# SwiGLU's upward products by seven half-depth products for two weight blocks and two token halves

## The chip, the cores and the metric

The kernel runs on one core of one Trainium2 chip. The metric is device time in microseconds (us) of one execution. Weights are read from device memory in every execution.

## The reference, cut to what matters

The program is one inference step of a two-layer decoder trunk, all in float32. There are 576 tokens: 512 of a prompt and 8 sequences of 8. Each layer has a SwiGLU block (FFN), a mixer and a second FFN; the model width is 1024 and the inner width of an FFN 2816.

```python
def swiglu(h, w1, w3, w2):
    return (jax.nn.silu(h @ w1) * (h @ w3)) @ w2

for l in range(DEPTH):                      # 2 layers
    ada = silu(c) @ w_ada + b_ada           # shift, scale, gate x 3
    h = modulate(rms_norm(x, g_ffn1), sh1, sc1)
    x = x + 0.5 * gt1 * swiglu(h, w1_a, w3_a, w2_a)
    h = modulate(rms_norm(x, g_mix), sh2, sc2)
    x = x + gt2 * mixer(h)                  # retention, two convolutions, gates
    h = modulate(rms_norm(x, g_ffn2), sh3, sc3)
    x = x + 0.5 * gt3 * swiglu(h, w1_b, w3_b, w2_b)
```

The change touches `h @ w1` and `h @ w3` of the four FFNs.

## The kernel before

Activations lie transposed: a tile has 128 features by 576 tokens, and the width of 1024 is eight such tiles, `self.h`. Tokens are worked in two halves of `HB` = 288 columns. Every float32 operand is held as a pair `hi`, `lo` of the type fp32r: `hi` is a rounded copy, made on ScalarE (ACT), and `lo` the rest, a subtraction on VectorE (DVE). A product is then three matmuls, `hi`·`hi`, `hi`·`lo` and `lo`·`hi`, into one PSUM bank (`three`, L210 to L212; the activations' `lo` comes second).

A weight block is 128 x 1024: 128 output features, all eight depth tiles beside each other. It has 48 matmuls: 8 depth tiles x 2 token halves x 3. An FFN has `FT` = 22 pairs of blocks upward, one of `w1` and one of `w3`; `post` forms silu of the first times the second, and splits the result into `ghi`, `glo`. After each of three `GROUPS` of pairs (6, 8 and 8), eight blocks of `w2` carry the group's part downward and add it to `x` (`residual`). The first pairs of an FFN are worked in `begin` (or `begin_first`), woven into the end of the normalisation before.

The order of work is written out by hand: `self.steps` is a list of steps with the weight blocks that each uses, and each engine carries out its instructions in the order in which the steps issue them. `pump` looks ahead in the list of weights: it issues the load of a raw block (on SP's queue) while fewer than `RAW` raw buffers are held, and splits the next raw block, ACT's copy (L161) and DVE's subtraction (`rest`, L121), while fewer than `WB` = 5 pairs of buffers are live and the block is at most `AHEAD` = 4 weight blocks away. It is called from `use`, and from `tick` between products. `spare` blocks are split into general slots instead. In the first and the second FFN, units of the matrix `w_ada` (two loads and eight matmul records a unit) are put between the steps (`add_fill`), with up to `ADA` = 12 of their loads ahead. GpSimd (POOL) adds the residual of the 64 sample tokens (L590) and takes small parts of the normalisation and the mixer.

## Time and profile before

| | |
|---|---|
| median of 3 runs | 3166.7 us (3166.56 to 3167.11) |
| the profiled execution's own time | 3166.99 us |
| its span, first to last instruction | 3165.2 us |
| TensorE matmul (PE) busy | 3104.3 us, 98% of the span |
| VectorE (DVE) busy | 1537.2 us, 49% |
| ScalarE (ACT) busy | 873.5 us, 28% |
| GpSimd (POOL) busy | 394.4 us, 12% |
| mean granted TensorE clock | 0.992 |

The profiled execution is one of the program on the chip. Busy time is the union of an engine's instructions. A matmul's record is longer than the distance to the next matmul, since they overlap; the number of matmuls in a stretch gives their distance. "PEld" is the load of a matmul's stationary operand.

### The profile page before, as it was taken

What the parts mean: (1) busy time and instruction counts of PE and PEld (TensorE: products, weight loads), DVE (VectorE), ACT (ScalarE), POOL (GpSimd) and SP (SyncE); (2) the same over time, 40 slices, a digit from 0 to 9 for tenths busy, and PEclk for the clock granted to TensorE, in tenths of its full rate; (3) what the DMA queues carried; (4) which work ended last, traced back from release to release, by engine and by line L of the source; (5) the groups of instructions that cost most, each with busy time, mean ns of one, the idle gap of its engine ahead of it and who ended that gap; (6) DMA issues with size and microseconds to landing.
All of it is one profiled execution on the core that took longest, in us unless ns stands there. A gap on an engine that the chain in (4) does not pass through costs nothing.

```text
span 3165.2 us, 55293 instructions
## 1 busy us (share of the span) xinstructions
PE 3104.3 (98%) x23412; PEld 2979.4 (94%) x23412; DVE 1537.2 (49%) x2840; ACT 873.5 (28%) x1468; POOL 394.4 (12%) x526
## 2 busy tenths in 40 slices
PE   7999999999999999999999999999998999999998
PEld 5999999899999999999999999988998999999998
DVE  5333336356985463323363333454579654533334
ACT  4222223222233342222232222332222333422221
POOL 1000004223112020000020000042221210200000
PEclk9999999999999999999999999999999999999999
DMA  7544423324222334636322222233342232222221
GB/s 274 166 154 150 150 94 123 110 75 117 72 84 84 107 121 136 208 133 212 112 80 78 86 86 86 85 118 113 89 112 64 83 101 89 77 85 85 81 81 57
DMA packets 142680, 349.67 MB, mean 110 GB/s; under 512 B 32400, under 2 KB 36752, under 8 KB 142432
## 3 DMA queue, kind: packets, MB, share of 16 engines
q1 hardware_dynamic: 135776, 329.35, 33.0%
q0 software_dynamic: 5504, 15.61, 1.8%
q8 instruction: 183, 3.00, 0.4%
q10 hardware_dynamic: 1152, 1.18, 0.1%
q14 instruction: 65, 0.53, 0.1%
HBM read 328.90 MB, written 12.45 MB: 108 GB/s over the span
## 4 chain that ended last, share of the span: by engine, by line
PE 87%; DVE 8%; POOL 2%; issue 1%; DMA 1%; ACT 1%; ACTq 0%; SPq 0%; DVEq 0%; POOLq 0%
PE pl L210 26%; PE pl L211 26%; PE pl L212 26%; DVE cv L957 4%; PE pm L277 2%; DVE lo L121 1%; PE pl L765 1%; PE pl L767 1%; PE pl L766 1%; PE pm L1164 1%; PE pm L1166 1%; DMA ada<-in_ada 1%; DVE cv L955 1%; DVE hl L383 0%; DVE t L393 0%
## 5 line engine op out<-in xcount | busy, mean ns | idle before, releaser
L210 PE MATMUL pl<-hh,hi 128*128 128x288 f32 x4576 | 1364.4, 298 | 9.3 <-DVE m L870 9.0
L211 PE MATMUL pl<-hl,hi 128*128 128x288 f32 x4576 | 1353.9, 296 | 10.1 <-POOL hl L421 9.6
L212 PE MATMUL pl<-hh,lo 128*128 128x288 f32 x4576 | 1353.1, 296 | 0.0
L210 PEld LDWEIGHTS pl<-hh,hi 128*128 128x128 f32 x4576 | 863.7, 189 | 32.3 <-DVE m L870 10.7
L211 PEld LDWEIGHTS pl<-hl,hi 128*128 128x128 f32 x4576 | 863.6, 189 | 12.7 <-POOL hl L421 10.9
L212 PEld LDWEIGHTS pl<-hh,lo 128*128 128x128 f32 x4576 | 863.4, 189 | 0.0
L121 DVE TENSOR_TENSOR lo<-raw,hi 128x1024 fp32r<-128x1024 f32 (+1 forms) x446 | 550.5, 1236 | 527.9 <-ACT hi L161 527.9
L161 ACT CAST hi<-raw 128x1024 fp32r<-128x1024 f32 (+1 forms) x446 | 459.0, 1032 | 845.5 <-PE pl L211 659.8
L210 PE MATMUL pl<-ghi,hi 128*128 128x288 f32 x1408 | 419.9, 298 | 0.0
L212 PE MATMUL pl<-ghi,lo 128*128 128x288 f32 x1408 | 415.2, 295 | 0.0
L211 PE MATMUL pl<-glo,hi 128*128 128x288 f32 x1408 | 415.1, 295 | 0.0
L210 PEld LDWEIGHTS pl<-ghi,hi 128*128 128x128 f32 x1408 | 264.4, 188 | 13.6 <-issue 11.5
L612 DVE TENSOR_TENSOR t<-t,pl 128x288 f32<-128x288 f32 x176 | 79.9, 454 | 404.7 <-PE pl L212 390.1
L590 POOL TENSOR_TENSOR xs<-xs,t 128x64 f32<-128x64 f32 x112 | 41.2, 368 | 1836.3 <-DVE t L587 1836.2
L211 PEld LDWEIGHTS pl<-glo,hi 128*128 128x128 f32 x1408 | 264.5, 188 | 0.0
L212 PEld LDWEIGHTS pl<-ghi,lo 128*128 128x128 f32 x1408 | 264.4, 188 | 0.0
L210 PE MATMUL pl<-s,hi 128*128 128x288 f32 x768 | 228.0, 297 | 1.9 <-DVE m L870 1.9
L211 PE MATMUL pl<-s,hi 128*128 128x288 f32 x768 | 226.6, 295 | 1.1 <-DVE s L226 1.1
L212 PE MATMUL pl<-s,lo 128*128 128x288 f32 x768 | 226.6, 295 | 0.0
L225 ACT CAST ghi<-t 128x288 fp32r<-128x288 f32 x176 | 76.1, 432 | 481.5 <-DVE t L612 481.5
L957 DVE SCALAR_TENSOR_TENSOR cv<-up,vec,cv 128x512 f32<-128x512 f32 x240 | 192.9, 804 | 5.4
L210 PEld LDWEIGHTS pl<-s,hi 128*128 128x128 f32 x768 | 144.4, 188 | 5.5 <-DVE m L870 2.4
(197 smaller groups left out, 2699.8 us busy)
## 6 DMA issues: line engine op xcount, KB each, us to landing
ada<-in_ada SPq DMA_DIRECT2D x288, 256.0 KB, 4.5
raw<-in_win SPq DMA_DIRECT2D x120, 512.0 KB, 3.6
raw<-in_w1a SPq DMA_DIRECT2D x44, 512.0 KB, 3.6
raw<-in_w3a SPq DMA_DIRECT2D x44, 512.0 KB, 3.6
raw<-in_w1b SPq DMA_DIRECT2D x44, 512.0 KB, 3.6
raw<-in_w3b SPq DMA_DIRECT2D x44, 512.0 KB, 3.6
raw<-in_w2a SPq DMA_DIRECT2D x32, 512.0 KB, 3.5
raw<-in_w2b SPq DMA_DIRECT2D x32, 512.0 KB, 3.5
```

Source lines behind the costliest of these rows:

```text
L121: self.nc.vector.tensor_sub(lo, t, hi.bitcast(F32))
L161: nc.scalar.copy(hi[:, :m], t[:, c])
L210: mm(ps[:, :HB], hi[:, c], x[0][:, t], start=first, stop=False)
L211: mm(ps[:, :HB], hi[:, c], x[1][:, t], start=False, stop=False)
L212: mm(ps[:, :HB], lo[:, c], x[0][:, t], start=False, stop=last)
L225: nc.scalar.copy(hi, src)
L277: nc.tensor.matmul(self.ps_ada[32 * j:32 * j + 32, :], self.cs[:, k], w, start=(k == 0), stop=(k == 7))
L590: nc.gpsimd.tensor_add(xs, xs, t[:].rearrange("p b t -> p (b t)"))
L612: nc.vector.tensor_mul(s, s, ps[1][:, :HB])
L765: mm(ps, xh, wh, start=(k == 0), stop=False)
L766: mm(ps, xh, wl, start=False, stop=False)
L957: nc.vector.scalar_tensor_tensor(cv[:, :S], up[:, k:k + S], w[:, k:k + 1], cv[:, :S], ALU.mult, ALU.add)
```

## The change

Two neighbouring weight blocks of the same kind and the two token halves are taken as a 2 x 2 by 2 x 2 product of blocks: weights by output block and by half of the depth, activations by half of the depth and by token half. Seven products of half depth (12 matmuls each) and sums before and behind them give what eight products of half depth (96 matmuls) gave.

- Pairs 0 and 1 stay as they were. Pairs 2 to 21 go two at a time through `duo_step`: `seven` for the two `w1` blocks, then `seven` for the two `w3` blocks. `GROUPS` are now 4, 6, 6 and 6 pairs.
- Weights: `sums` forms three sums from the raw blocks `a` and `b` on POOL (four adds of 128 x 512, and one of the four in a buffer `s1` of which there is one), and `halves` splits what came of them: X, Z and Y of 128 x 1024 and S of 128 x 512, each into one of the `WB` = 5 pairs of buffers. They are `jobs`, issued one at a time by `pump` when a pair of buffers is free.
- Activations: `forms` makes sums of the activations once for each FFN (POOL, DVE and ACT), `last_forms` overwrites a quarter of `hh`, `hl` with the last of them.
- Behind the products: `post` is called for each of the four results with one or two operands; sums on DVE, the three later products of the gate on POOL.
- Buffers: `RAW` 3 to 4, slots 38 to 37, temporary tiles 12 to 10; loads of `w_ada` ahead 12 to 4 after the start (`ADA_LATER`). `TAPS` in the mixer's convolution goes from 3, 1, 4 to 2, 2, 4; the mean in its norm uses another constant.

```diff
-GROUPS = ((0, 6), (6, 8), (14, 8))
+GROUPS = ((0, 4), (4, 6), (10, 6), (16, 6))
-RAW, WB, AHEAD, ADA = 3, 5, 4, 12
+RAW, WB, AHEAD, ADA, ADA_LATER = 4, 5, 4, 12, 4
-TAPS = 3, 1, 4
-SLOTS, TEMPS = 38, 12
+TAPS = 2, 2, 4
+SLOTS, TEMPS = 37, 10
...
-                if self.whole < ADA and self.n_dma <= self.cur + 2 * ADA:
+                if self.whole < (ADA if self.quota < 9 else ADA_LATER) and self.n_dma <= self.cur + 2 * ADA:
...
-            if self.raw and self.quota and self.order[self.raw[0][0]] <= self.order[self.cur] + AHEAD:
+            if self.jobs:
+                if self.live < WB:
+                    self.jobs.popleft()()
+                    if not later:
+                        self.rest()
+                    went = True
+            elif self.raw and self.quota and self.order[self.raw[0][0]] <= self.order[self.cur] + AHEAD:
                 key = self.keys[self.raw[0][0]]
                 spare = key in self.spare
-                if spare or self.live < WB:
+                if key in self.duo:
+                    if len(self.raw) > 1:
+                        self.sums(key, self.raw.popleft()[1], self.raw.popleft()[1])
+                        went = True
+                elif spare or self.live < WB:
...
+    def halves(self, key, t, n=1024):
+        w = [self.wp.tile([128, 1024], F32R, tag=x, bufs=WB, name=self.name(x)) for x in ("hi", "lo")]
+        self.live += 1
+        self.nc.scalar.copy(w[0][:, :n], t[:, :n])
+        self.late.append((w[1][:, :n], t[:, :n], w[0][:, :n]))
+        self.split[key] = w
+
+    def sums(self, key, a, b):
+        add = self.nc.gpsimd.tensor_add
+        s = self.wp.tile([128, 512], F32, tag="s1", bufs=1, name=self.name("s1"))
+        add(s, b[:, :512], b[:, 512:])
+        add(b[:, :512], b[:, :512], a[:, :512])
+        def z():
+            self.rest()
+            add(a[:, :512], a[:, :512], s)
+            add(a[:, 512:], a[:, 512:], a[:, :512])
+            self.halves((*key, "Z"), a)
+            self.held -= 1
+        def y():
+            self.halves((*key, "Y"), b)
+            self.held -= 1
+        self.jobs.extend((lambda: self.halves((*key, "X"), a), z, y, lambda: self.halves((*key, "S"), s, 512)))
+
+    def part(self, key, which):
+        self.cur = max(self.cur, self.at[key])
+        self.pump()
+        return self.split[(*key, which)]
...
+    def forms(self):
+        ...
+        for i in range(4):
+            za, zb = self.slot([128, NT], what="za"), self.slot([128, NT], what="zb")
+            nc.gpsimd.tensor_add(za, self.hh[:, i, :NT].bitcast(F32), self.hl[:, i].bitcast(F32))
+            nc.gpsimd.tensor_add(zb, self.hh[:, i + 4, :NT].bitcast(F32), self.hl[:, i + 4].bitcast(F32))
+            yield
+            a, b = slice(0, HB), slice(HB, NT)
+            nc.vector.tensor_sub(za[:, a], za[:, a], za[:, b])
+            nc.vector.tensor_sub(za[:, b], za[:, b], zb[:, b])
+            nc.vector.tensor_add(zb[:, b], zb[:, b], za[:, a])
+            nc.vector.tensor_sub(zb[:, a], zb[:, b], zb[:, a])
+            t5 = self.slot([128, NT], F32R, "t5")
+            hi, lo = self.slot([128, NT], F32R, "thi"), self.slot([128, NT], F32R, "tlo")
+            nc.scalar.copy(hi, zb)
+            nc.scalar.copy(t5[:, a], za[:, a])
+            yield
+            nc.vector.tensor_sub(lo, zb, hi.bitcast(F32))
+            nc.vector.tensor_sub(t5[:, b], za[:, a], t5[:, a].bitcast(F32))
+            ...
+            yield
...
+    def seven(self, key, post):
+        ...
+        def product(ps, which, at, xs, first, last):
+            hi, lo = self.part(key, which)
+            for i, x in enumerate(xs):
+                c = slice(512 * at + 128 * i, 512 * at + 128 * i + 128)
+                k = dict(skip_group_check=True)
+                mm(ps, hi[:, c], x[0], start=first and i == 0, stop=False, **k)
+                mm(ps, hi[:, c], x[1], start=False, stop=False, **k)
+                mm(ps, lo[:, c], x[0], start=False, stop=last and i == 3, **k)
+        ...
+        p = bank()
+        product(p, "X", 0, quarter(0, 0), True, True)
+        s1 = self.temp([128, HB])
+        nc.scalar.copy(s1, p)
+        q = bank()
+        product(q, "Z", 0, self.T[2], True, True)
+        u, v = self.temp([128, HB]), s1
+        nc.vector.tensor_sub(u, s1, q)
+        product(p, "X", 1, quarter(1, 0), False, True)
+        free("X")
+        post(0, 0, p)
+        product(q, "Y", 0, self.T[7], False, True)
+        nc.vector.tensor_sub(v, s1, q)
+        r = bank()
+        product(r, "S", 0, self.T[5], True, True)
+        free("S")
+        post(1, 1, v, r)
+        t = bank()
+        product(t, "Y", 1, self.T[4], True, True)
+        free("Y")
+        post(1, 0, v, t)
+        product(r, "Z", 1, quarter(1, 1), False, True)
+        free("Z")
+        post(0, 1, u, r)
+        self.pump()
...
+        def duo_step(f):
+            ...
+            def up1(i, j, a, b=None):
+                t = self.temp([128, HB])
+                if b is None:
+                    nc.scalar.activation(t, a, AF.Silu)
+                else:
+                    if i == 0:
+                        nc.vector.tensor_add(t, a, b)
+                    else:
+                        nc.vector.scalar_tensor_tensor(t, a, -1.0, b, ALU.mult, ALU.subtract)
+                    nc.scalar.activation(t, t, AF.Silu)
+                acts[i, j] = t
+            def up3(i, j, a, b=None):
+                s = acts.pop((i, j))
+                if b is None:
+                    nc.vector.tensor_mul(s, s, a)
+                else:
+                    t = self.temp([128, HB])
+                    ...   # the same sum as in up1, into t
+                    nc.gpsimd.tensor_mul(s, s, t)
+                ...
+                nc.scalar.copy(hi, s)
+                waiting.append(lambda: nc.vector.tensor_sub(lo, s, hi.bitcast(F32)))
+            ...
+            self.seven(pairs[f][0], up1)
+            self.seven(pairs[f][1], late)     # late: up3, then the subtractions waiting from before
...
+                    if f % 2 == 0:
+                        ks = [pairs[f][0], pairs[f + 1][0], pairs[f][1], pairs[f + 1][1]]
+                        self.steps.append((ks, lambda f=f: duo_step(f)))
+                        add_fill(4)
```

## Rows read from the trace of the kernel before

**Rows 1.** The page: busy time of each engine, share of the span, instructions.

```profile
PE 3104.3 (98%) x23412; PEld 2979.4 (94%) x23412; DVE 1537.2 (49%) x2840; ACT 873.5 (28%) x1468; POOL 394.4 (12%) x526
```

**Rows 2.** Stretches of the third FFN: length, PE, PEld, DVE, ACT, POOL, clock, DMA.

```profile
1750.00:1800.00 50.00, 50.00 (x379) 50.00 (x379) 16.97 (x25) 13.27 (x21) 0.65 (x2) 1.00 0.30 92
1800.00:1850.00 50.00, 50.00 (x380) 50.00 (x379) 17.11 (x24) 14.35 (x24) 0.00 (x0) 1.00 0.27 78
```

**Rows 3.** Groups by shape, ACT and DVE: count, busy us, mean ns, idle before.

```profile
L161 ACT CAST hi<-raw 128x1024 fp32r<-128x1024 f32 x414 | 432.3, 1047 | 775.7 <-PE pl L211 620.1 <-PE pl L761 51.1 <-issue 37.7
...
L121 DVE TENSOR_TENSOR lo<-raw,hi 128x1024 fp32r<-128x1024 f32 x414 | 519.3, 1256 | 501.1 <-ACT hi L161 501.1
...
L161 ACT CAST w<-raw 128x512 fp32r<-128x512 f32 x20 | 10.9, 616 | 0.0
...
L121 DVE TENSOR_TENSOR w<-raw,w 128x512 fp32r<-128x512 f32 x20 | 12.5, 686 | 0.0
...
L611 ACT ACTIVATE t<-pl 128x288 f32<-128x288 f32 x176 | 71.5, 406 | 169.0 <-PE pl L212 169.0
...
L612 DVE TENSOR_TENSOR t<-t,pl 128x288 f32<-128x288 f32 x176 | 79.9, 454 | 404.7 <-PE pl L212 390.1 <-ACT t L611 14.5
...
L225 ACT CAST ghi<-t 128x288 fp32r<-128x288 f32 x176 | 76.1, 432 | 481.5 <-DVE t L612 481.5
...
L226 DVE TENSOR_TENSOR s<-sv,s 128x576 fp32r<-128x576 f32 x8 | 6.0, 754 | 2.2 <-ACT s L225 2.1
```

**Rows 4.** The same groups on POOL: two inputs in SBUF.

```profile
L421 POOL TENSOR_TENSOR hl<-s,hh 128x512 fp32r<-128x512 f32 x5 | 6.3, 1261 | 0.0
...
L414 POOL TENSOR_TENSOR s<-s,ada 128x512 f32<-128x512 f32 x5 | 5.6, 1120 | 0.4
...
L411 POOL TENSOR_TENSOR s<-xs,t 128x512 f32<-128x512 f32 x5 | 9.1, 1815 | 23.1 <-ACT t L409 23.1
...
L974 POOL TENSOR_TENSOR s<-cv,cv 128x576 f32<-128x576 f32 x2 | 2.8, 1424 | 0.0
...
L704 POOL TENSOR_TENSOR s<-t,t 128x288 f32<-128x288 f32 x16 | 13.2, 824 | 113.6 <-DVE t L700 113.6
```

**Rows 5.** The timeline of `post` (start us, us): DVE's product, ACT's copy, DVE's subtraction.

```profile
1201.53 0.46 DVE L612 TENSOR_TENSOR t<-t,pl 128x288 f32<-128x288 f32 x1 [3.21 <-PE pl L212]
...
1202.02 0.43 ACT L225 CAST ghi<-t 128x288 fp32r<-128x288 f32 x1 [3.29 <-DVE t L612]
...
1202.49 0.46 DVE L226 TENSOR_TENSOR glo<-t,ghi 128x288 fp32r<-128x288 f32 x1 [0.50 <-ACT ghi L225]
```

**Rows 6.** The timeline of two places where DVE and POOL work together.

```profile
1156.03 1.21 DVE L121 TENSOR_TENSOR lo<-raw,hi 128x1024 fp32r<-128x1024 f32 x1
1156.18 1.23 POOL L590 TENSOR_TENSOR xs<-xs,t 128x64 f32<-128x64 f32 x1 [17.56 <-DVE t L587]
...
809.08 7.77 DVE L955 TENSOR_SCALAR cv<-up,vec 128x512 f32<-128x512 f32 x1
809.55 7.01 POOL L949 TENSOR_TENSOR tap<-us,vec 128x496 f32<-128x496 f32 x6
```

**Rows 7.** The one line of POOL's residual add: duration ns min/median/max.

```profile
L590 POOL TENSOR_TENSOR xs<-xs,t x112: 310/322/1232, 129.3 to 3151.5; 128x64 f32<-128x64 f32 x112
```

**Rows 8.** The timeline: two units of `w_ada` on PE.

```profile
1207.68 1.07 PE L277 MATMUL pm<-ada,cs 128*32 128x256 f32 x16
```

**Rows 9.** The timeline of the opening of the second FFN: PE waits for POOL.

```profile
1180.71 0.40 PE L211 MATMUL pl<-hl,hi 128*128 128x288 f32 x1 [1.76 <-POOL hl L421]
```

**Rows 10.** A stretch as in rows 2, and PE's timeline in it, after a wait.

```profile
820.00:825.00 5.00, 3.79 (x21) 3.79 (x22) 4.93 (x7) 0.00 (x0) 2.05 (x2) 0.78 0.27 96
...
821.21 0.40 PE L210 MATMUL pl<-hh,hi 128*128 128x288 f32 x1 [2.98 <-DVE m L870]
...
823.23 0.45 PE L211 MATMUL pl<-hl,hi 128*128 128x288 f32 x1
823.47 0.44 PE L212 MATMUL pl<-hh,lo 128*128 128x288 f32 x1
```

More of the change, by code (lines that the diff above doesn't have):

```diff
@@ L114, in start @@
         self.order = np.cumsum([k[0] not in ("ada", "do") for k in self.keys]).tolist()
-        self.raw, self.late, self.split = deque(), deque(), {}
+        self.raw, self.late, self.split, self.jobs = deque(), deque(), {}, deque()
         self.n_dma = self.held = self.whole = self.live = self.cur = 0
@@ new lines, in last_forms @@
+    def last_forms(self):
+        for i, z in enumerate(self.zs):
+            hi, lo = self.T[7][i]
+            self.nc.scalar.copy(hi, z[:, HB:])
+            self.nc.vector.tensor_sub(lo, z[:, HB:], hi.bitcast(F32))
+        self.zs = None
+    def seven(self, key, post):
+        nc = self.nc
+        mm = nc.tensor.matmul
+        h = [(x[0][:, :NT], x[1]) for x in self.h]
+        quarter = lambda k, j: [(x[0][:, j * HB:(j + 1) * HB], x[1][:, j * HB:(j + 1) * HB]) for x in h[4 * k:4 * k + 4]]
+        def product(ps, which, at, xs, first, last):
[6 more added lines that the diff above has]
+                mm(ps, lo[:, c], x[0], start=False, stop=last and i == 3, **k)
+        bank = lambda: self.lin(HB)
+        free = lambda which: self.free((*key, which))
+        p = bank()
[23 more added lines that the diff above has]
+        self.pump()
@@ L467, in outer, with begin @@
         return ps
-    def begin(self, l, sh, pairs, post):
+    def begin(self, l, sh, pairs, post, forms=False):
         st = {}
@@ L493, in begin @@
         post(pairs[1], 0, self.outer(ws, 0, {0: spread, 1: first, 3: more, 5: more}))
-        for pair in pairs:
-            ps = self.outer([self.use(k) for k in pair], 1)
+        g = self.forms() if forms else iter(())
+        more = lambda: next(g, None)
+        for n, pair in enumerate(pairs):
+            hooks = {k: more for k in (1, 2, 3, 4, 5, 6)}
+            ps = self.outer([self.use(k) for k in pair], 1, hooks)
             for k in pair:
@@ L499, in begin @@
             post(pair, 1, ps)
+        if forms:
+            for _ in g:
+                pass
+            self.last_forms()
     def row(self, dg):
@@ L622, in ffn @@
         if not first:
-            self.spare |= {pairs[0][1], pairs[1][0]}
+            self.spare |= {pairs[0][1]}
+        for f in range(2, FT, 2):
+            for i in range(2):
+                self.duo[pairs[f][i]] = pairs[f + 1][i]
         def opening():
@@ L628, in opening @@
             else:
-                self.begin(l, sh, pairs[:2], post)
+                self.begin(l, sh, pairs[:2], post, True)
         def pair_step(pair):
@@ L640, in pair_step, with one_pair, late @@
                 post(pair, half, ps)
+        def one_pair():
+            self.bg.append(self.forms())
+            pair_step(pairs[1])
+            self.drain()
+            self.last_forms()
+        def duo_step(f):
+            nc = self.nc
+            self.ada_done()
+            for i in range(2):
+                g[f + i] = (self.slot([128, NT], F32R, "ghi"), self.slot([128, NT], F32R, "glo"))
+            acts = {}
+            def up1(i, j, a, b=None):
[15 more added lines that the diff above has]
+                    t = self.temp([128, HB])
+                    if i == 0:
+                        nc.vector.tensor_add(t, a, b)
+                    else:
+                        nc.vector.scalar_tensor_tensor(t, a, -1.0, b, ALU.mult, ALU.subtract)
+                    nc.gpsimd.tensor_mul(s, s, t)
+                c = slice(j * HB, (j + 1) * HB)
+                hi, lo = (x[:, c] for x in g[f + i])
+                nc.scalar.copy(hi, s)
+                waiting.append(lambda: nc.vector.tensor_sub(lo, s, hi.bitcast(F32)))
+            waiting = []
+            def late(i, j, a, b=None):
+                before = list(waiting)
+                waiting.clear()
+                up3(i, j, a, b)
+                for fn in before:
+                    fn()
+            self.seven(pairs[f][0], up1)
+            self.seven(pairs[f][1], late)
+            for fn in waiting:
+                fn()
+            if f + 2 == FT:
+                self.T = None
         def down(keys, final):
+            self.ada_done()
             f0, n = GROUPS[keys[0][3]]
@@ L663, in ffn @@
                     self.steps.append((ks, opening))
-                elif f > 1 or first:
-                    self.steps.append((pairs[f], lambda f=f: pair_step(pairs[f])))
-                    add_fill(0 if first and f == 5 else 2)
-            final = gi == 2
+                elif f > 1:
+                    if f % 2 == 0:
+                        ks = [pairs[f][0], pairs[f + 1][0], pairs[f][1], pairs[f + 1][1]]
+                        self.steps.append((ks, lambda f=f: duo_step(f)))
+                        add_fill(4)
+                elif first:
+                    self.steps.append((pairs[1], one_pair))
+                    add_fill(4)
+            final = gi == len(GROUPS) - 1
             if final:
```

18 lines of the change are left out of this document (13 added, 5 removed).

## The prediction, made before the result was known

> **What bounds the kernel now.** I read the page's busy shares first: PE is busy for 98% of the span, DVE for 49%, ACT 28%, POOL 12% [rows 1]. Busy PE alone proves little, so next the stretches of an FFN: 379 or 380 matmuls in every 50 us, PE never idle, clock 1.00 [rows 2]. That is 0.1316 us a matmul and 12.6 us a pair of weight blocks (96). The groups by shape come last, since they price what the change adds: the two halves of a split [rows 3] and what POOL needs for an add with two inputs [rows 4]. So an FFN is bound by PE today, and everything else hides behind it because splits run several blocks ahead. The reader should keep both halves of that: fewer matmuls help only while the splits stay ahead.
>
> **What it removes.** For two blocks `seven` issues 7 x 12 = 84 matmuls instead of 96. Ten duos x 2 kinds x 12 x 4 FFNs = 960 fewer of 23412; at 0.1316 us [rows 2] that is 126.3 us, if PE stays the bound. A duo (two pairs) would take 168 x 0.1316 = 22.1 us instead of 25.3, and one `seven` 11.05 us.
>
> **What it adds: a loop outside PE.** Each `seven` needs four POOL adds of 512, ACT copies of 3 x 1024 + 512, DVE subtractions of the same sizes, and more sums behind PE. By total, ACT and POOL fit. But engines keep the issued order, so I follow the queues. With five pairs of buffers, four hold the block in work and one the next block's X. After each `free` one job of the next block is issued, between the posts of the block in work:
>
> - ACT: Z copy, silu(1,1), Y copy, silu(1,0), S copy, silu(0,1), X copy of the block after next.
> - DVE: u, Z rest, v, sum(1,1), Y rest, sum(1,0), S rest, sum(0,1), X rest.
> - POOL: two adds for Z, then the first two adds of the block after next.
>
> Every entry waits for the one in front on its own queue, so they chain. The two adds for Z overwrite what the X rest reads and wait for it. Z copy waits for them, Z rest for the copy; v and sum(1,1) stand behind Z rest on DVE; silu(1,1) waits for that sum and Y copy stands behind silu; likewise through Y rest, sum(1,0), silu, S copy, S rest. `s1` has one buffer, so the next add waits for S rest; the X rest of the block after next is ready during the second add and must let POOL finish (below); it releases the next two adds. Nothing of PE is in this chain, and no queue may skip it.
>
> Its length in a `w1` block: four POOL adds at 1.26 (nearest shape, [rows 4]) 5.04; two copies at 1.05 and one at 0.62, 2.71; rests 3 x 1.26 + 0.69 = 4.46; three DVE ops at 0.45, 1.36; two silus at 0.41, 0.81 [rows 3]. Together 14.4 us against PE's 11.05. In a `w3` block three POOL products join (0.82 each, [rows 4], 2.47). The last of them stands in POOL's queue behind both first adds, so ACT's copy of its result (0.43) and the X copy (1.05) come onto the chain too: 18.4 us. A duo takes 32.8 us by the chain, 7.5 more than before. Hand-overs between engines, 0.03 to 0.04 us each [rows 5], some 37 of them, are partly paid back where ops on one queue overlap by 0.1 us; I take 33.4. PE is then idle a third of a duo.
>
> DVE's rests and POOL's adds also disturb each other: a POOL add of 64 columns, 0.32 us at the median [rows 7], took 1.23 beside a DVE rest and ended 0.17 us after it, and a DVE op took 7.77 us while POOL ran six products back to back [rows 6]. One waits for the other. If they exclude each other fully, POOL's 8 x 1.26 + 3 x 0.82 = 12.6 us and DVE's two-input ops, 6 x 1.26 + 2 x 0.69 + 4 x 0.46 = 10.8, make 23.4 us a duo. The chain is longer than this without it, so I price it only where an X rest meets the second add, which is in the sum above.
>
> **Where the chain starts late.** During downward steps the first block's four parts and the second's X are made, so the first duo of a group still runs near PE's pace. I go through a group of three duos from its start: the second block's X1 ends at 17.2 us (11.05 + 4.74 if unhindered, and 1.4 late, since u stands behind the X rest of the third). Blocks 2 to 4 take the chain, 18.4 + 14.4 + 18.4 = 51.2; block 5 lacks the sums for a successor, about 12.8; from X1 of the sixth four products remain, 6.3; hand-overs about 2.9. That is 90.4 us, before 75.8: +14.5. The group of one duo takes about 23.3 instead of 25.3: -2.0. An FFN without `w_ada` units: 3 x 14.5 - 2.0 = +41.5.
>
> With units between duos (first and second FFN) loads are issued in the order of the list and only four of the `w_ada` loads may be ahead, so the raw blocks behind eight of them are issued after the duo's last post. The next duo starts behind it on ACT, POOL and DVE: sum 0.45, POOL product 0.82, copies 0.43 and 1.05, then X rest after POOL's first adds (5.2 us from PE's end), adds, Z copy, Z rest at 10.2 us; PE has 2 us of units (two take 1.07, [rows 8]) and the X product to fill that. I get 35.3 us from duo to duo, 2 of it units, against 27.3: +8.0. The first duo of a group gains 2.9, and the downward step after a group waits 2.5. Three groups of three: -2.9 + 16 + 2.5 = +15.6; with the short group -0.4: +46.4 an FFN.
>
> Four FFNs: 2 x 41.5 + 2 x 46.4 = +176, PE's gain already in it.
>
> **The openings.** `forms` costs POOL eight adds of 576 at 1.42 [rows 4], 11.4 us, and DVE per i four ops of 288 at 0.45, one of 576 at 0.75 and one of 288 at 0.46 [rows 3], 12.2 us. Most of both have two inputs in SBUF, so I take them one after the other, 23.6. Cover: the second token half of pairs 0 and 1, 12.6, and X's product 1.6. The Z product waits about 10 us in three FFNs. In the first FFN the splits of the first duo stand behind `forms` too: about 14. Also, `pump` at the head of `begin` now reaches the first duo, and job z flushes the rests that `later` kept back, ahead of the statistics; PE already waits there for POOL at the end [rows 9]. Four rests of 1.26 give 5 us, three times. Together 44 + 15 = +59; bounds 0 (jobs not ready by then) and 100.
>
> **Moved and small.** Loads: 512 KB blocks stay as many, in smaller groups for `w2`; residual posts grow by a third, hidden behind PE where it is busy. TAPS, the fourth group and the shorter products in `end` I cost at nothing, +-10 us: conv steps stay on DVE and only change places; were DVE's cover gone, PE would wait as in the stretch at 820 us [rows 10].
>
> **Sum.** 3166.99 (profiled execution; 0.29 above the median) + 176 + 59 = 3402; I say 3400. Bounds on the chain: eight POOL adds at 1.12 as in the cheapest row of 512 [rows 4], -1.1 a duo, and no hand-overs, -0.6; for the 24 duos that are not first in a group -41, and openings at nothing, -59: 3300. Adds at 1.82 (the dearest row, [rows 4]): +4.5 a duo, +108, and openings +41: 3550. I take 1.26, the row with the same shape and two plain inputs, because the chain itself keeps DVE's rests apart from most adds.
>
> **Rivals.**
> 1. The chain is as above, and PE falls to its lower level as well. After an idle 2.98 us PE ran at granted 0.78 and its matmuls came 0.24 us apart, level 1.2 GHz, for a few us [rows 10]. Waits at least as long are to come in each block, but PE has 2 to 3 us to spare behind each. If it stayed low throughout, a duo would be 168 x 0.24 = 40.3 us: 24 x 6.9 = +166, 3570.
> 2. Faster: the side engines keep pace and only the exclusion of DVE and POOL counts. It decides if the chain per block closes under 11.05 us, which needs v and the sums to run ahead of Z rest. A duo at 23.4 then gives 40 x -1.9 = -76, with openings +59: 3150. By PE alone: -126 + 59: 3100. For it: DVE is half idle today [rows 1], and rows 6 show the exclusion itself. Against: the order on DVE's queue. The Trainium skill (SBUF — State Buffer, section "SBUF: two separate sides") has the exclusion as a rule: a DVE op with two SBUF inputs and a GpSimd op hold the shared port pair for their whole length, and the other blocks. By that rule, as the trace agrees in rows 6, the sum would be this rival's 3150.
> 3. No change: the chain is half as harmful as I think; 24 x 8.1 us of loss halved and openings at nothing leave about 3167.
> 4. The matmul count doesn't fall: the diff leaves no room for it.
>
> **Chances.** Forecast 0.80; rival 1 0.07; rival 2 0.10 (0.07 and 0.03); rival 3 0.03. Faster by over 0.2% 0.10, within 0.2% (6 us, about what a measurement can tell from no change) 0.03, slower 0.87. The range, 3230 to 3580, holds forecast and rival 1 with their bounds, and a chain somewhat cheaper than its lower bound; it leaves out rivals 2 and 3.
>
> **What would show it.** 22452 matmuls. PE's share falls to near 88%, with gaps of 3 us and over in duos, most before X1, released by ACT's copy of the first result. DVE's v ends right after Z rest, Z rest after Z copy, Z copy after two POOL adds; the first add of a block starts after S rest. 33 us from duo to duo in the third and fourth FFN. Wrong would be: PE at 380 matmuls in 50 us inside duos, or Z rest done before Y0's product ends.

## The result, and the profile after

The changed kernel takes 3631.0 us (median; 3623.75 to 3635.9), 1.1462 times the time before (95% interval 1.1444 to 1.148): slower by 464 us, where 233 were forecast and the range ended at 3580. Its profiled execution took 3631.74 us, with a span of 3629.9.

The page's busy shares, as in [rows 1]:

```profile
PE 3132.2 (86%) x22452; PEld 2956.4 (81%) x22452; DVE 1965.4 (54%) x3517; ACT 1052.1 (29%) x1785; POOL 1026.8 (28%) x1029
```

The 960 matmuls are gone, and PE is busy 28 us longer. Next the second FFN (with `w_ada` units) and the third (without), as stretches (columns as in [rows 2]); first the kernel before, then the changed one. An FFN is cut here, and in the table further down, where POOL starts the last subtraction of each opening (L421 before, L472 after); the first counts from the start, the fourth to the end of the span.

```profile
1179.40:1650.70 471.30, 469.31 (x3786) 442.02 (x3786) 175.04 (x320) 120.11 (x202) 25.18 (x44) 1.00 0.46 151
1650.70:2077.10 426.40, 424.33 (x3192) 423.82 (x3192) 170.74 (x294) 119.52 (x201) 24.58 (x44) 1.00 0.27 84
```

```profile
1320.30:1959.40 639.10, 491.32 (x3540) 447.05 (x3539) 284.31 (x488) 165.10 (x281) 180.00 (x170) 0.87 0.33 113
1959.40:2465.40 506.00, 426.28 (x2975) 415.03 (x2973) 277.98 (x466) 164.59 (x283) 173.26 (x166) 0.92 0.23 72
```

In the third FFN PE idles 79.7 us, before 2.1, and what 217 fewer recorded matmuls saved was paid back: busy 426.3 us against 424.3, at a granted clock of 0.92. The second FFN, equal but for its units, lost 168 us instead of 80. The two mixers, the rest of the span, took 663 us each before and after. What PE waited for, over the whole span (us in total, times, longest):

```profile
PE pl L529 <- ACT t L538: 154.4, 52, 7.0
PE pm L344 <- DVE t L333: 118.9, 17, 15.2
PE pl L529 <- ACT thi L497: 34.4, 9, 11.7
PE pm L328 <- DMA ada<-in_ada: 24.0, 15, 8.1
PE pl L529 <- ACT t L752: 20.8, 3, 7.8
PE pm L401 <- DVE t L394: 17.8, 5, 5.8
```

L529 are the matmuls of `seven`; in the first row they are X's second half, waiting for ACT's copy of the first product: the forecast's loop. L344 are the transposes of a finished block of `w_ada`; the forecast has no such wait. The rows with L497 and L752 belong to the first duos, the one with L401 to the statistics of the normalisation. The loop in the timeline of the third FFN, from S's rest to the next duo:

```profile
2061.89 0.69 DVE L129 TENSOR_TENSOR lo<-s,hi 128x512 fp32r<-128x512 f32 x1 [1.02 <-ACT hi L193]
2062.66 1.27 POOL L203 TENSOR_TENSOR s<-raw 128x512 f32<-128x512 f32 x1 [8.10 <-DVE lo L129]
2064.01 1.27 POOL L204 TENSOR_TENSOR raw<-raw,raw 128x512 f32<-128x512 f32 x1
2064.39 1.97 DVE L129 TENSOR_TENSOR lo<-raw,hi 128x1024 fp32r<-128x1024 f32 x1 [1.44 <-ACT hi L193]
2066.51 1.28 POOL L208 TENSOR_TENSOR raw<-raw,s 128x512 f32<-128x512 f32 x1 [1.23 <-DVE lo L129]
2067.87 1.28 POOL L209 TENSOR_TENSOR raw<-raw 128x512 f32<-128x512 f32 x1
2069.18 1.05 ACT L193 CAST hi<-raw 128x1024 fp32r<-128x1024 f32 x1 [0.58 <-POOL raw L209]
2070.27 1.22 DVE L129 TENSOR_TENSOR lo<-raw,hi 128x1024 fp32r<-128x1024 f32 x1 [2.13 <-ACT hi L193]
...
2072.33 0.45 DVE L825 TENSOR_TENSOR glo<-t,ghi 128x288 fp32r<-128x288 f32 x1
2072.49 0.95 POOL L821 TENSOR_TENSOR t<-t,t 128x288 f32<-128x288 f32 x1 [3.35 <-DVE t L820]
...
2076.56 0.95 POOL L821 TENSOR_TENSOR t<-t,t 128x288 f32<-128x288 f32 x1 [3.12 <-DVE t L820]
...
2079.30 1.26 POOL L203 TENSOR_TENSOR s<-raw 128x512 f32<-128x512 f32 x1 [1.79 <-DVE lo L129]
...
2081.96 0.78 POOL L821 TENSOR_TENSOR t<-t,t 128x288 f32<-128x288 f32 x1
...
2084.51 0.61 PE L529 MATMUL pl<-hh,hi 128*128 128x288 f32 x1 [6.88 <-ACT t L538]
2084.91 0.44 PE L530 MATMUL pl<-hl,hi 128*128 128x288 f32 x1
2085.15 0.44 PE L531 MATMUL pl<-hh,lo 128*128 128x288 f32 x1
...
2096.89 1.28 POOL L203 TENSOR_TENSOR s<-raw 128x512 f32<-128x512 f32 x1 [8.63 <-DVE lo L129]
```

Read it as the forecast told it: S rest, two adds, X rest, two adds for Z, Z copy, Z rest. From first add to first add one turn is 2079.30 - 2062.66 = 16.6 us and the next 17.6; a duo 34.2, forecast 33.4. The first of these turns holds two of a `w3` block's POOL products (L821), the second the last of them, which stands behind both first adds, so they are not the forecast's 14.4 and 18.4 one by one. POOL's add takes 1.27 (taken: 1.26, [rows 4]). After the 6.88 us that PE stood, its matmuls come 0.24 us apart, twice the 0.1316 of [rows 2], as in [rows 10].

### The profile page after: what moved, and what is told of

Its sections match the earlier page's. It is cut to its first block, busy times and chain, and to the rows that moved or that the text cites. A ratio compares the mean times of both kernels' runs of the same rounds, so it can differ in the third digit from the quotient of the medians.

```text
span 3629.9 us, 55455 instructions
## 1 busy us (share of the span) xinstructions
PE 3132.2 (86%) x22452; PEld 2956.4 (81%) x22452; DVE 1965.4 (54%) x3517; ACT 1052.1 (29%) x1785; POOL 1026.8 (28%) x1029
## 5 line engine op out<-in xcount | busy, mean ns | idle before, releaser
L129 DVE TENSOR_TENSOR lo<-raw,hi 128x1024 fp32r<-128x1024 f32 (+2 forms) x561 | 694.1, 1242 | 875.3 <-ACT hi L193 472.6
L263 PE MATMUL pl<-hh,hi 128*128 128x288 f32 x2064 | 617.7, 299 | 0.3 <-ACT hh L470 0.2
L264 PE MATMUL pl<-hl,hi 128*128 128x288 f32 x2064 | 612.0, 296 | 6.4 <-POOL hl L472 3.9
L265 PE MATMUL pl<-hh,lo 128*128 128x288 f32 x2064 | 611.0, 296 | 0.0
L529 PE MATMUL pl<-hh,hi 128*128 128x288 f32 x1280 | 416.3, 325 | 186.7 <-ACT t L538 154.4
L179 ACT CAST hi<-raw 128x1024 fp32r<-128x1024 f32 (+2 forms) x321 | 300.0, 939 | 640.1 <-PE pl L264 306.2
L529 PEld LDWEIGHTS pl<-hh,hi 128*128 128x128 f32 x1280 | 265.0, 207 | 213.6 <-ACT t L538 169.4
L531 PE MATMUL pl<-hh,lo 128*128 128x288 f32 x1280 | 401.1, 313 | 7.4 <-DVE lo L129 7.4
L530 PE MATMUL pl<-hl,hi 128*128 128x288 f32 x1280 | 401.8, 314 | 0.0
L264 PEld LDWEIGHTS pl<-hl,hi 128*128 128x128 f32 x2064 | 390.6, 189 | 8.6 <-POOL hl L472 4.6
L263 PEld LDWEIGHTS pl<-hh,hi 128*128 128x128 f32 x2064 | 390.8, 189 | 5.2 <-issue 3.0
L265 PEld LDWEIGHTS pl<-hh,lo 128*128 128x128 f32 x2064 | 390.3, 189 | 0.0
L193 ACT CAST hi<-raw 128x1024 fp32r<-128x1024 f32 x240 | 248.2, 1042 | 271.5 <-POOL raw L209 189.8
L531 PEld LDWEIGHTS pl<-hh,lo 128*128 128x128 f32 x1280 | 264.4, 207 | 8.6 <-DVE lo L129 8.6
L821 POOL TENSOR_TENSOR t<-t,t 128x288 f32<-128x288 f32 x120 | 107.5, 899 | 559.2 <-DVE t L820 550.2
```

The costliest lines, as they stand in the source:

```text
L129: self.nc.vector.tensor_sub(lo, t, hi.bitcast(F32))
L179: nc.scalar.copy(hi[:, :m], t[:, c])
L193: self.nc.scalar.copy(w[0][:, :n], t[:, :n])
L263: mm(ps[:, :HB], hi[:, c], x[0][:, t], start=first, stop=False)
L264: mm(ps[:, :HB], hi[:, c], x[1][:, t], start=False, stop=False)
L265: mm(ps[:, :HB], lo[:, c], x[0][:, t], start=False, stop=last)
```

## The experiments

Stage lengths are us between the cuts named above. Ratios are to the kernel before, with 95% intervals; its median beside these runs was 3165.7 to 3167.4.

| run | median | ratio | FFN 1 | FFN 2 | FFN 3 | FFN 4 |
|---|---|---|---|---|---|---|
| before (profiled: 3167.0) | 3166.7 | 1 | 516 | 471 | 426 | 426 |
| after | 3631.0 | 1.146 (1.144 to 1.148) | 658 | 639 | 506 | 501 |
| e1 settings alone | 3169.8 | 1.001 (1.000 to 1.002) | 523 | 474 | 431 | 425 |
| e2 adds early | 3633.4 | 1.148 (1.146 to 1.150) | 660 | 636 | 506 | 502 |
| e3 rests late | 3518.8 | 1.112 (1.110 to 1.113) | 635 | 615 | 470 | 467 |
| e4 no `w_ada` loads | 3541.3 | 1.119 (1.117 to 1.120) | 623 | 582 | 506 | 502 |
| e5 = e3, W3 product on DVE | 3437.2 | 1.086 (1.084 to 1.087) | 623 | 597 | 446 | 441 |
| e6 two buffers for S | 3601.0 | 1.137 (1.135 to 1.139) | 656 | 635 | 494 | 489 |
| e7 transposes later | 3591.5 | 1.134 (1.132 to 1.136) | 640 | 620 | 506 | 502 |
| e8 no `forms` | 3449.5 | 1.090 (1.088 to 1.091) | 597 | 561 | 486 | 478 |
| e9 `forms` adds on DVE | 3621.4 | 1.144 (1.142 to 1.145) | 659 | 636 | 503 | 498 |
| e10 = e8, slots held | 3544.4 | 1.119 (1.117 to 1.121) | 637 | 616 | 486 | 479 |
| e11 = e5 + e7 | 3380.6 | 1.068 (1.066 to 1.069) | 598 | 578 | 443 | 441 |
| e12 = e11, plain first pairs | 3295.3 | 1.041 (1.039 to 1.042) | 568 | 549 | 432 | 429 |
| e13 = e12, five groups | 3220.2 | 1.017 (1.016 to 1.019) | 536 | 503 | 434 | 429 |
| e14 = e12, no `w_ada` loads | 3212.5 | 1.015 (1.013 to 1.016) | 539 | 493 | 433 | 429 |
| e15 = e12, sevens in FFN 3, 4, `ADA_LATER` 8 | 3175.5 | 1.003 (1.002 to 1.004) | 522 | 474 | 432 | 429 |
| e16 = e15, adds on POOL | 3178.1 | 1.004 (1.002 to 1.005) | 521 | 474 | 435 | 430 |
| e17 = e15, sums earlier, other groups | 3135.4 | 0.990 (0.989 to 0.992) | 517 | 471 | 414 | 416 |
| e18 = e17, adds on POOL | 3135.2 | 0.990 (0.989 to 0.992) | 517 | 471 | 415 | 415 |

**e1: the shared settings alone**, in the kernel before.

```diff
-GROUPS = ((0, 6), (6, 8), (14, 8))
-RAW, WB, AHEAD, ADA = 3, 5, 4, 12
-TAPS = 3, 1, 4
-SLOTS, TEMPS = 38, 12
+GROUPS = ((0, 4), (4, 6), (10, 6), (16, 6))
+RAW, WB, AHEAD, ADA, ADA_LATER = 4, 5, 4, 12, 4
+TAPS = 2, 2, 4
+SLOTS, TEMPS = 37, 10
...
```

> The kernel before with the change's shared settings alone (four groups of 4, 6, 6, 6 pairs instead of 6, 8, 8; four raw buffers instead of three; at most 4 tiles of w_ada on their way instead of 12; 37 slots and 10 temporaries instead of 38 and 12; the transfer shares 2, 2, 4; one spare weight in slots instead of two), all of its 24 matmuls per product kept. Theory A (the forecast was missed in the two FFNs with w_ada units because the smaller look-ahead starves the units, whatever the products are): 3250 to 3330, the extra 80 to 180 us all in the first two FFNs. Theory B (the seven products' chain through DVE, ACT and POOL is the cause, and the settings matter only together with it): 3160 to 3210; a fourth round of downward products costs no more matmuls, only eight more residual updates per FFN, off PE.

Theory B: 4 us. They are the sum of two shifts: the FFNs are 7, 2, 5 and 0 us longer, the two mixers 5 us shorter each (658 and 657 instead of 663). The short look-ahead for `w_ada` costs little while PE runs plain pairs.

**e2: Z's two additions queued right behind X's rest**, a part earlier.

```diff
-            self.rest()
-            add(a[:, :512], a[:, :512], s)
-            add(a[:, 512:], a[:, 512:], a[:, :512])
             self.halves((*key, "Z"), a)
...
+        def x():
+            self.halves((*key, "X"), a)
+            self.rest()
+            add(a[:, :512], a[:, :512], s)
+            add(a[:, 512:], a[:, 512:], a[:, :512])
...
```

> The changed kernel with the two POOL additions that make Z issued together with X's copy and rest, one part earlier than Z's copy, so that ACT no longer stands still behind them; every instruction is kept. Theory of the queues' order (ACT waits 2.5 us in each block for two additions of 1.27 us, with SiLU and the next copies behind it): about 5 us less in each duo that is longer than 25 us, some 30 of them: 3450 to 3560. Rival, the exclusion of DVE and POOL (the same seconds of both on one port): within 20 us of 3631. Rival, PE's lower clock: within 20 us of 3631.

Nothing, so the expectation failed. PE's wait before X's second half in this kernel, and the place in the timeline:

```profile
PE pl L532 <- ACT t L541: 154.9, 52, 7.0
```

```profile
2061.27 1.97 DVE L129 TENSOR_TENSOR lo<-raw,hi 128x1024 fp32r<-128x1024 f32 x1 [1.45 <-ACT hi L193]
2063.38 1.28 POOL L209 TENSOR_TENSOR raw<-raw,s 128x512 f32<-128x512 f32 x1 [1.23 <-DVE lo L129]
```

The addition still starts when X's rest has ended, after the same 1.23 us, wherever it is queued: here nothing else stood in front of it.

**e3: the rests behind the sums that SiLU waits for.** In `seven`, `pump(True)` leaves a rest waiting until the next `post` has put its DVE work in the queue.

```diff
-        self.pump()
+        self.pump(True)
+        if (*key, which) in self.new:
+            self.rest()
...
         post(1, 1, v, r)
+        self.rest()
...
         post(1, 0, v, t)
+        self.rest()
...
         post(0, 1, u, r)
+        self.rest()
```

> The changed kernel with DVE's rests (lo = sum - hi) of the four parts not queued at once behind ACT's copy but after the next sums that SiLU waits for; every instruction is kept. Theory of the queues' order (sums and SiLU stand behind rests that wait for ACT): the block's chain of 14.4 and 18.4 us falls to 10.5 and 12.9, below PE's 25 us for a duo, so 5 to 8 us less in each of some 30 duos: 3390 to 3500. Rivals, exclusion of DVE and POOL or PE's lower clock: within 20 us of 3631, since no work is taken away.

112 us less with every instruction kept, where the rivals, as written, had 20 at most; 19 us short of the expected range, and 20 of the waits before X's second half stayed (96.2 us). One of them, POOL's and PE's timeline:

```profile
2053.29 0.95 POOL L829 TENSOR_TENSOR t<-t,t 128x288 f32<-128x288 f32 x1 [1.52 <-DVE t L828]
2056.74 1.26 POOL L206 TENSOR_TENSOR s<-raw 128x512 f32<-128x512 f32 x1 [2.50 <-DVE lo L130]
2058.08 1.26 POOL L207 TENSOR_TENSOR raw<-raw,raw 128x512 f32<-128x512 f32 x1
2059.30 0.79 POOL L829 TENSOR_TENSOR t<-t,t 128x288 f32<-128x288 f32 x1
...
2061.86 0.61 PE L534 MATMUL pl<-hh,hi 128*128 128x288 f32 x1 [5.26 <-ACT t L543]
```

The last product of a duo (2059.30) stands behind two additions for the next weights, and ACT's copies behind it: the step that the forecast has in its `w3` chain.

**e5: that product on DVE**, on top of e3.

```diff
-                    nc.gpsimd.tensor_mul(s, s, t)
+                    nc.vector.tensor_mul(s, s, t)
```

> The kernel of the run with late rests, and in it the three products SiLU times upward of each W3 block (0.79 to 0.96 us on POOL) moved to DVE (where one of this size takes 0.46 us). Theory of the queues' order: with late rests TensorE's wait for the copy of the first product, 20 times 4.8 us, stands behind ACT's copy of the last product of the duo before, and that behind a POOL product queued after two additions for the next weights (they wait for S's rest); with the product on DVE both additions pass it by, the 20 waits go, and with each some 1.4 us of slow matmuls after it: 3370 to 3430. Rival, DVE's and POOL's shared time: DVE gets 1.4 us more in each W3 block of 11 us and POOL loses it, no gain: 3500 to 3540.

82 us less, 7 short of the expected bound. The wait, 96.2 us in 20 places in e3, is now:

```profile
PE pl L534 <- ACT t L543: 29.8, 20, 3.9
```

DVE carries the products besides, and the third FFN is still 24 us shorter: DVE's total was not the bound. The run does not separate the product's place, no longer behind two additions, from its length, 0.46 us instead of 0.79 to 0.95.

**e6: two buffers for S**, `bufs=2`.

> The changed kernel with two buffers for S instead of one (and 8 temporaries instead of 10, to make room). The forecast's chain holds the step S's rest, then the first addition for the next block (260 us of POOL's waiting in 46 places); with a second buffer that addition waits for nothing but the raw weights. Theory of the forecast's chain, link by link: about 3 us less in each of some 30 duos: 3530 to 3580. Rival: the addition only has to be early enough for its in-order neighbours, and the rest, placed ahead of the sums, keeps the duo at 33 us: within 25 us of 3631. Rival, DVE's and POOL's shared time: within 25 us of 3631.

30 us, between the theories: 12 us in each FFN without units, 2 and 4 in the others. POOL's wait moved on by one link, from the first addition (L203, 260.1 us in 46 places) to Z's (L208, 212.4 in 48), which needs X's rest.

**e4: no loads of `w_ada` after the opening.**

```diff
-                    self.split[key] = self.slot([128, 512], what="ada")
-                    nc.sync.dma_start(self.split[key], self.source(key)[0])
+                    if self.quota < 9:
+                        self.split[key] = self.slot([128, 512], what="ada")
+                        nc.sync.dma_start(self.split[key], self.source(key)[0])
+                    else:
+                        self.split[key] = self.vec[:, :512]
```

> The changed kernel with the w_ada tiles of all units after the opening not loaded: the units multiply a tile that is resident (other numbers in the modulations), so their loads and their slots are gone, their matmuls, copies and transposes stay. Theory A (the loads of w_ada wait for slots in SP's queue, with the raw weights behind them): 100 to 180 us less, 3450 to 3530, all in the first two FFNs, and their duos as long as those of the third and fourth, 34 us with the units' own 2. Theory B (the transposes that wait for DVE's copy behind a block of rests): within 40 us of 3631, and PE's waits at the transposes stay near 119 us.

Between both: 90 us, all in the first two FFNs, while 82.4 of the 119 us at the transposes stayed.

**e7: the transposes between a duo's two blocks.**

```diff
-            self.ada_done()
...
             self.seven(pairs[f][0], up1)
+            self.ada_done()
             self.seven(pairs[f][1], late)
...
```

> The changed kernel with the transposes of a finished block of w_ada queued between a duo's two blocks instead of at its head (and in a downward step after its first half), so that DVE's copy, which stands behind a block of rests, has a block's time; every instruction is kept. Theory A, the wait is paid in full: the 119 us at the transposes go, 3500 to 3530. Theory B, the wait is partly a loan: the duo after a wait takes 25.1 us instead of 33 to 34, since its parts are then ready, so of 11.8 us about 4 remain to be gained: 3570 to 3610. Rival, not on the path: within 15 us of 3631.

Theory B. The wait falls from 118.9 us to

```profile
PE pm L344 <- DVE t L333: 12.1, 3, 9.4
```

and the time by 40. The rest had been a loan: while PE stood, the side engines caught up, and the next duo ran without a wait. The fourth duo of the first FFN, behind a wait of 11.8 us in the changed kernel, took 24.9 us there and 32.7 in e7. A sum of waits says how long an engine stood, not what their removal brings.

**e8, e10: no `forms`; then with the slots that it holds.** In e8 `T` holds plain quarters of `h`. e10 adds

```diff
+        self.hold = [self.slot([128, NT], what="room") for _ in range(12)]
+        for t in self.hold:
+            nc.gpsimd.memset(t[:, 0:1], 0.0)
...
```

> The changed kernel without the sums of the token halves (T2, T4, T5, T7 are plain quarters of h; the products have other values): 8 POOL additions, 24 DVE and 12 ACT instructions fewer in each of the four openings. Theory (the first duo takes 46 to 50 us instead of 33 to 36 because the halves' sums come late, and the opening waits behind them on POOL and DVE): 12 to 20 us less in each FFN, 3550 to 3585. Rival (the first duo is long because the first raw weights and their sums come late, whatever the tokens): within 20 us of 3631.

> The kernel of the run without the halves' sums, in which twelve of the 37 slots are held to the end of each FFN's last duo by buffers that nothing uses (a memset and a copy of one column each), as the halves' sums hold them. That run was 182 us faster than the changed kernel: 61 and 78 us in the two FFNs with w_ada units and 20 and 23 in the others. Theory of room (in the first two FFNs the slots that the sums hold make w_ada's loads wait, and raw weights behind them in SP's queue): the first two FFNs lose 30 to 50 us each again, 3510 to 3550. Rival (it is the instructions alone that cost, their order and their stay ahead of the first duo): 3445 to 3470.

181.5 us less without them, and 95 of these come back with the slots alone, 41 and 54 in the first two FFNs, 0 in the others. SP's queue in the second FFN shows how; first after, then e8, then e10:

```profile
SPq L143 <- PE pm L328: 222.7, 41, 36.3
```

```profile
SPq L143 <- PE pm L328: 73.7, 18, 15.4
```

```profile
SPq L143 <- PE pm L328: 236.1, 41, 36.5
```

L143 are the loads of `w_ada`, waiting for a slot that PE's units must empty; raw weights queue behind them. Part of it reaches PE at the transposes (L344), whose wait is 82.2 us in e8 and 119.7 in e10. The other 87 us are the sums' instructions: 20, 23, 20 and 22 us an FFN.

**e9: the eight additions of `forms` on DVE.** The first opening of the changed kernel showed DVE's subtractions beside POOL's additions, and after them:

```profile
80.62 1.61 POOL L487 TENSOR_TENSOR za<-hh,hl 128x576 f32<-128x576 f32 x1
81.08 1.47 DVE L492 TENSOR_TENSOR za<-za,zb 128x288 f32<-128x288 f32 x1
...
90.54 0.46 DVE L492 TENSOR_TENSOR za<-za,zb 128x288 f32<-128x288 f32 x1
```

The DVE instruction with two inputs stood until POOL's had ended. The Trainium skill (SBUF — State Buffer, section "SBUF: two separate sides") has this as an exclusive lock, and the trace agrees: 1.47 instead of 0.46.

> The changed kernel with the eight additions h = hi + lo of the token halves' sums in each opening on DVE instead of POOL (576 columns: 1.61 to 2.4 us each on POOL; DVE took 0.75 us for one of that size). In the first opening DVE's subtractions of 288 columns took 1.47 to 1.65 us between 79 and 89 us, while POOL added, and 0.46 after it. Theory of shared time (a DVE instruction stands until POOL's has ended): the halves' sums end some 10 us earlier in each of the four openings: 3570 to 3600. Rival (their length is that of the steps of the hooks and of the order of ACT and DVE, or DVE, with 6 us more work, is the bound): 3620 to 3650.

The rival: 10 us. In e9 DVE does the additions itself (0.75 us for most of them), and in the first opening its last step of the sums ends at 96.65 us instead of 99.37. The lock is real, but the time that DVE stood is nearly made up by the additions that it has now.

**e11 to e14: together, and the first two FFNs.** e11 is e5 with e7. e12 makes the first four pairs plain, puts the sums under the first downward steps, and multiplies S third. e13 has five groups and `ADA_LATER` 8; e14 is e12 with e4's edit.

```diff
+        def plain(f):
+            pair_step(pairs[f])
+            if f == 3:
+                self.bg.append(self.forms())
...
-GROUPS = ((0, 4), (4, 6), (10, 6), (16, 6))
+GROUPS = ((0, 4), (4, 4), (8, 4), (12, 4), (16, 6))
```

> The kernel with late rests and the W3 products on DVE (3437), with the transposes of w_ada between a duo's blocks as well. In the changed kernel that move gained 40 us of 119, since the duo after a wait was shorter. With the chain gone, a duo takes 25.6 us whether or not a wait stood ahead of it, so now the wait is paid in full, with the slow matmuls after it. Theory of the loan: 3335 to 3375, 60 to 100 us less, all in the first two FFNs. Rival (the gain stays what it was there): 3390 to 3405.

> All that gained, and the first two duos' place changed: the first four pairs of each FFN are plain products, the halves' sums (all on DVE) are made during the first downward steps, and S is multiplied third, ahead of X's second half, so that the copy of the first product has two products' time. TensorE gets 24 matmuls more in each FFN than with ten duos. Theory (what the halves' sums cost at the opening, up to 182 us, is cover that was lacking, and the downward steps have it; the waits of 1.1 and 1.7 us left in each duo go): 3150 to 3230, near the kernel before. Rival (their cost is DVE's work or their room in the slots): 3280 to 3350.

> The kernel with plain first pairs (3295) with five groups of 4, 4, 4, 4, 6 pairs instead of 4, 6, 6, 6, so that the first four hold 8 slots for the gated activations instead of 12, and at most 8 tiles of w_ada on their way instead of 4. Theory of room (the 130 us left in the two FFNs with w_ada units are loads that wait for slots): 3200 to 3250, all of it there; a fifth round of downward products costs the other two some 2 us each. Rival (the units' work itself, their copies and transposes): 3285 to 3315.

> The kernel with plain first pairs (3295) without w_ada's loads after the opening (the units multiply a resident tile; other modulations). In the changed kernel this gained 90 us. Theory of room and queue: all that is left goes but the opening of the first FFN, 3165 to 3215. Rival (units' work between the duos, or the transposes): 3250 or more.

e11: 57 us from the move that gave 40 alone, 6 short of the expected range. e12: 85, in the rival's range; its three edits were not run apart. e13 points to room: with four fewer slots for activations and twice the tiles on their way, together, it takes 75 off, nearly as much as no loads at all (83).

**e15 to e18: the sevens only where no units are.** e15 and e16 put them in the last two FFNs. e17 and e18 begin the sums two pairs earlier and have groups of 4, 4, 6, 8.

```diff
+        strassen = not fill
...
-            if f == 3 and strassen:
+            if f == 2 and strassen:
                 self.bg.append(self.forms())
...
-GROUPS = ((0, 4), (4, 6), (10, 6), (16, 6))
+GROUPS = ((0, 4), (4, 4), (8, 6), (14, 8))
```

> The kernel with plain first pairs, with the seven products only in the two FFNs without w_ada units (9 duos each, 432 matmuls fewer in all than the kernel before) and plain pairs in the other two, 8 tiles of w_ada on their way. By the stages measured so far (3rd and 4th FFN 432 and 429 us against 426 and 425; settings alone 4 us): 3175 to 3190. Rival (the work that one stage leaves for the next grows or shrinks with its neighbours): outside this.

> The same with the additions of the halves' sums on POOL, as in the changed kernel, while the downward products run. Under the downward products TensorE waits 5.5 and 3.5 us for DVE's residual updates, with the halves' sums queued among them; eight additions of 0.75 us leave DVE. Theory of queue order: 5 us less in each of the two FFNs, 3160 to 3180, about the kernel before. Theory of shared time (DVE's subtractions take 1.5 us beside POOL's additions of 1.6): equal to the run before or up to 10 us slower.

> The kernel with seven products in the last two FFNs only (3175), with the halves' sums begun one stage earlier, under the third and fourth plain pairs (25 us more of cover; their last part, T7, under the first downward steps), and with groups of 4, 4, 6, 8 pairs, so that the last is as long as in the kernel before. Theory of cover: the waits of 5.5, 3.5 and 2 us at the first downward steps and duo go, twice some 10 us, and 2.7 us at the changes of stage: 3145 to 3162, faster than the kernel before. Rival (DVE's work, wherever it stands, sets that stretch, and eight pairs of activations leave no free slot beside the sums): 3170 to 3190.

> The same with the eight additions of the halves' sums on POOL. Theory of cover: DVE has 6 us less to do in the stretch, and with 50 us of cover its stands beside POOL's additions (eight of 1.6 us) cost nothing: equal to the run before or up to 5 us faster. Theory of shared time: DVE's sums stand 1.5 us instead of 0.46 beside POOL's, 0 to 10 us slower than the run before.

e15 came out as the stages said; whether POOL or DVE adds makes next to no difference (2.6 us more in e16, 0.2 less in e18). e17 beats the kernel before by 31.6 us, 10 more than its theory's best. Not all of it comes from the sevens: the third and fourth FFN are 23 us shorter than before, and 9 lie in the mixers, which take 658 us each here (663 before, 658 and 657 in e1). PE's waits from the third FFN's first plain pairs to its first duo, e15 and then e17:

```profile
PE pl L268 <- DVE x L731: 9.7, 3, 5.5
PE pl L535 <- ACT t L544: 2.0, 1, 2.0
```

```profile
PE pl L268 <- DVE x L738: 1.7, 1, 1.7
PE pl L542 <- ACT t L551: 1.4, 1, 1.4
```

e17's third FFN as a stretch:

```profile
1645.50:2059.00 413.50, 398.71 (x2978) 394.51 (x2977) 279.89 (x490) 157.79 (x277) 132.70 (x123) 1.00 0.27 88
```

PE is busy 26 us less than before there, at clock 1.00, and idle 15 instead of 2. The two edits of e17 were not run apart; the first two FFNs, where the groups alone differ from e15, are 5 and 3 us shorter too.

## Why the prediction was wrong

**The loop outside PE** held, sign by sign: 22452 matmuls, PE at 86% (named: near 88), the largest share of its waiting before X's second half (154.4 us), the first add behind S's rest, 34.2 us from duo to duo. So did the group of three duos: 93.9, 91.0 and 92.8 us in the third FFN, forecast 90.4. e3 shows that it is order, not work: 112 us went with every instruction kept, and e5's move of the products took 82 more. That speaks against the exclusion of rival 2 as the bound; "no queue may skip it" was true of the queues as issued only.

**The step that failed for size is FFNs with units, "+46.4 an FFN".** With the opening, 60 and 61 us were forecast; measured are 142 and 168. The forecast took the raw loads behind `w_ada`'s as a delay at each duo, 8.0 us, and the units as 2 us. It missed that the units' own tiles have no room: the sums hold twelve of 37 slots to the end of an FFN (e10 against e8: 41 and 54 us). And it has no price for `ada_done` at the head of `duo_step`: its transposes wait for a copy that stands behind a block of rests on DVE (e7: 17 and 20 us). The two overlap, since the transposes' wait falls with the slots freed as well (e8).

**The openings, "44 + 15 = +59"**: the 44 were half of what came. Without the sums' instructions the four FFNs are 20, 23, 20 and 22 us shorter (e10 against after), 87 in all (unrounded). The first duo of the third FFN took 45.5 us, forecast some 33. The wait itself was priced about right: before the tiles of Z's product PE stands 5.4, 3.1 and 2.2 us there, 10.8 in all, forecast 10; over the four FFNs (rows L497 and L752 above) 55 us, forecast 44. What the forecast left out is what follows it: 3.9 us before X's second half, and the lower clock. The duo as a stretch:

```profile
1974.70:2020.00 45.30, 28.89 (x168) 26.39 (x167) 29.78 (x47) 15.38 (x31) 10.34 (x7) 0.74 0.11 30
```

Its 168 matmuls keep PE busy 28.9 us instead of 22.1, at a granted clock of 0.74. The 15 us for rests ahead of the statistics came: PE stands 5.8, 2.8 and 5.8 us before L401 in the openings of the second, third and fourth FFN, and not at all there before. In the second:

```profile
1305.10 4.05 DVE L129 TENSOR_TENSOR lo<-raw,hi 128x1024 fp32r<-128x1024 f32 x2 [0.41 <-ACT hi L179]
1309.07 0.14 DVE L390 TENSOR_SCALAR t<-pm 96x3 f32<-96x3 f32 x1
...
1313.79 1.17 PE L401 MATMUL pm<-t,ones 96*128 96x96 f32 x4 [5.83 <-DVE t L394]
```

It is two rests of together 4 us, beside POOL's additions, and not four of 1.26. By the cuts used here, two of these three waits fall into the mixers, which are 5 and 6 us longer than in e1; the settings' gain there hides them.

By these cuts 60, 61, 51.5 and 51.5 us were forecast for the four FFNs. With the miss by FFN 81, 106, 28 and 24 us, room, transposes and sums account for 65, 87, 10 and 12 if they add, which e4, e7, e8 and e11 show they do only roughly. Of the remaining 16, 19, 18 and 12, the groups of three give 6.5 in the third FFN (3.5, 0.6 and 2.4 over the forecast), and the settings, costed at nothing, 7, 2, 5 and 0 with plain pairs (e1); what makes up the rest stays open.

**Rival 1**, the lower clock, was no rival but a part: granted 0.87 to 0.92 in the FFNs, and in the third PE's whole saving of busy time was gone. It stays with the waits: e17, whose waits are short, has 1.00 there. **Gain of PE, "126.3"**: the count fell as forecast. e17, with 432 fewer matmuls, could save 432 x 0.1316 = 56.9 us and saves 23 in the two FFNs that have them. **Rival 3**'s sum was wrong: half of 24 x 8.1 us and the openings off 3402 leave 3246, inside the range, and not 3167.

## What to carry to other kernels

Trading matmuls for sums pays only as long as every added instruction has cover: look for the queue in which it stands in front of something that PE needs, and put it behind that; such a move took 112 us here, and taking a product out of POOL's queue 82 more. Count room as a price: a buffer held through a stage takes it from the loads that ran ahead there, and the loss appears on another queue. And use such a scheme only where other loads do not need the same room and queues: in all four FFNs seven products cost 14.6% as written and 1.7% in the best order tried; with them in two FFNs the kernel was 1.0% faster, and 0.7% lies in these two FFNs.

## What the runs showed of the hardware

- After a wait of 11.82 us PE's granted clock was 0.50, the level of 1.2 GHz, in the next 3 us, and its matmuls came 0.24 us apart. The Trainium skill (TensorE: Matmul & The Clock Gate, section "HAM oscillation — how this bites in real kernels") says that a kernel which waits again and again starts each burst at the low clock; the trace agrees:

```profile
243.60:246.60 3.00, 2.90 (x13) 2.90 (x14) 1.47 (x3) 0.00 (x0) 2.84 (x3) 0.50 0.00 0
```

```profile
243.70 0.69 PE L344 MATMUL pm<-ident,t 128*128 128x128 f32 x2 [11.82 <-DVE t L333]
244.04 0.59 PE L529 MATMUL pl<-hh,hi 128*128 128x288 f32 x1
244.43 0.44 PE L530 MATMUL pl<-hl,hi 128*128 128x288 f32 x1
244.67 0.44 PE L531 MATMUL pl<-hh,lo 128*128 128x288 f32 x1
```

- A POOL product of 288 columns took 0.95 us beside DVE and 0.79 alone, a DVE subtraction 1.47 beside POOL and 0.46 alone; moving all eight additions off POOL still gained only 10 us of 3631.
